# The first two modulation rows moved from TensorE to VectorE, stepped from the third attention's projections on, and five weight buffers instead of six

## The chip, the cores and the metric

One core of a Trainium2 chip runs the kernel. The metric is the device time of one execution in microseconds (us); the kernel before takes 2123.35 us, the median of three runs from 2120.63 to 2124.16 us. TensorE multiplies matrices into PSUM, VectorE and ScalarE do the elementwise work, GpSimd a few masks and small operations, and SyncE issues nearly all of the DMA transfers from one queue, in order.

## The reference, cut to what matters

Two stacks of two layers follow each other on one sequence of 256 tokens with 1024 channels. A layer of the first stack has a state-space branch, three attention branches and gates over them, and a SwiGLU feed-forward block. A layer of the second stack has a gated mixer, differential attention against 256 further context tokens, and a convolutional feed-forward block; its norms are shifted and scaled by "modulation" vectors. What the change touches is how these vectors are computed. They depend on nothing but two inputs, `c` and `c_ctx`, and on weights, so they can be computed at any time before the second stack:

```python
def adaln(cvec, w, b, n):
    m = jax.nn.silu(cvec) @ w[:, : n * D_MODEL] + b[: n * D_MODEL]
    return jnp.split(m, n, axis=-1)

for l in range(DEPTH):
    cmod = adaln(c_ctx, w_mod[l], b_mod[l], 2 if last else 6)
    sh1, sc1, g1, sh2, sc2, g2 = [m[:, None, :] for m in adaln(c, w_mod[l], b_mod[l], 6)]
```

For each of two layers that is a product of two vectors of 1024 (one for the latent tokens, one for the context) with a matrix of 1024 x 6144, in six rows of 1024 outputs.

## The kernel before, in words

All large products run in three passes over operands that are split into a high and a low half (`mm3`, lines 508 to 510). The weights come as a stream of units of at most 128 x 1024 numbers, 512 KB (`Stream`, lines 245 to 292): `_load` (line 258) issues the DMA on SyncE's queue into one of `RAW` = 6 buffers named raw, `_split` (line 266) makes the high half hi on ScalarE (line 275) and the low half lo on VectorE (line 277), each in one of four buffers, and TensorE then multiplies. The load is thus queued until the low half of the unit six places before has been made.

Work that isn't on the main line of projections is written as generators. `run_side` (line 475) takes one step of each of the "lanes" (the attention branches and the like) between projections. The modulation is one more generator, `mods` (line 1117), advanced by `fill` (line 493); `spread` (line 500) counts steps and calls `fill` at each `every`-th of them, while fewer than `goal` fills are done. A tile scheduler then orders the instructions of each engine by a simulated clock, with the order of writing as the priority, so an instruction may run far ahead of its place in the code.

`mods` goes through 6 rows x 8 steps for each layer. A step loads 128 x 1024 modulation weights, 512 KB, into one of two buffers named wm (line 1141, SyncE's queue, one step ahead). Rows 0 and 1 of the first layer, called early, are summed on TensorE: four matmuls a step with 32 columns each, of which two are not zero, into four groups of PSUM partitions (line 1159), over eight steps. All other rows are summed on VectorE, in two halves of 512 and for each of the two vectors (one vector in the last rows of the second layer): first a product (line 1170), then seven multiply-adds (line 1172) into a tile macc. `mod_end` (line 1183) finishes a row: for the rows of VectorE TensorE first sums macc over the partitions by eight matmuls with a vector of ones (line 1190); then for every row a copy, two transposes (line 1198) and an addition of the bias (line 1202), in later steps.

In `first_layer` (line 625) for l = 0 the sixteen steps of the early rows are advanced at each second gate product (lines 750 and 751), four for each of four gates, and two more steps, the first two of row 2, behind the gates (lines 774 and 775). The second layer's norm needs rows 0 and 1 first in `ctx_norm` (line 1604), right behind. The feed-forward block and the output product then take a step at every second unit. The third attention is the branch with the projections fq, fk and fv (lines 701 to 703).

Of the kernel before, what the change touches and what calls it, by code (L numbers as in the profile page):

```python
# [9 lines left out]
F32 = mybir.dt.float32  # L10
FR = mybir.dt.float32r
AF = mybir.ActivationFunctionType
ALU = mybir.AluOpType
# [13 lines left out]
UNIT = 1024  # L27
GROUP = {n: g for g, ns in (("a", "sm p pt dp at on yo osq"), ("c", "cth lj cn"), ("g", "gz gsq gu ga"), ("m", "mo"))
         for n in ns.split()}
KEEP = 1154 + 4 + 64 + 2 * (280 + 80 + 96 + 48)  # L30
LIM = 2.4e19
# [264 lines left out]
class Kern:  # L296
    RAW = 6
    CPINS = (None, None, None, 0, None, None, None, 1)
# [16 lines left out]
    SIDE2 = 5  # L315
    MSTEP = 1
    WM = 2
# [7 lines left out]
    def __init__(self, nc, tc, ctx, dr, stop=None):  # L325
        self.nc, self.tc, self.dr = nc, tc, dr
        self.stop = stop
        e = ctx.enter_context
        self.cp = e(tc.tile_pool(name="const", bufs=1))
        self.wp = e(tc.tile_pool(name="wts", bufs=4))  # L330
        self.sp = e(tc.tile_pool(name="slots", bufs=self.NSLOT))
        self.tp = e(tc.tile_pool(name="tmp", bufs=3))
        self.mp = e(tc.tile_pool(name="psmm", bufs=4, space=PSUM))
        self.ap = e(tc.tile_pool(name="psax", bufs=4, space=PSUM))
        self.dp = e(tc.tile_pool(name="scratch", bufs=1, space=bass.MemoryType.DRAM))
        self.x = self.cp.tile([128, 2, D], F32, name="x")
        self.xc = self.cp.tile([128, 2, D], F32, name="xc")
        cpk = const_params()
        kept = self.cp.tile([128, cpk.n + KEEP], F32, name="kept")
        self.kept, self.kept_n = kept, 0  # L340
        self.ident, cst, self.tabs, self.ctp, self.ct, self.ones, self.nh, self.par_f = (
            self.keep(n) for n in (128, cpk.n, 512, 256, 16, 1, 1, 240))
        self.cst_all, self.cst = cst, {n: cpk.get(cst, n) for n in cpk.at}
        for t in range(2):
            for h in range(2):
                sl = slice(512 * h, 512 * h + 512)
                nc.sync.dma_start(self.x[:, t, sl], dr["x"][128 * t:128 * t + 128, sl])
        nc.sync.dma_start(self.ident, dr["ident"])
        nc.gpsimd.memset(self.ones, 1.0)
        nc.gpsimd.memset(self.nh, -0.5)  # L350
        self.par = {}
        self.uid = 0
        self.lanes = [[] for _ in range(7)]
        self.front = []
        self.P2, self.late, self.ctx_out, self.tails = None, [], {}, []
        self.filler, self.filled = None, 0
        self.steps, self.every, self.goal = 0, 0, 51
        layers = [(dr[f"w_f{l}"], first_units(l)) for l in range(2)] + [(dr[f"w_s{l}"], second_units(l)) for l in range(2)]
        self.st = Stream(self, layers)
# [114 lines left out]

    def run_side(self, n=1):
        for lane in self.lanes:
            for _ in range(n):
# [48 lines left out]
    def proj_N(self, key, acts, width, k0=0, per=2, side=1, kbs=None, ps=None, last=True, held=0, pins=()):  # L526
# [25 lines left out]
        for kb in kbs[:len(kbs) - held]:  # L552
            some(self.st.next(key + (k0 + kb,)), kb, range(nt))
            self.run_side(side)
            self.spread()
        if held:
# [68 lines left out]
    def first_layer(self, x, x4, l, done=None):  # L625
        nc = self.nc
# [60 lines left out]
        for n, (a, b, c) in ((3, ("dq", "dk", "dv")), (2, ("mq", "mk", "mv"))):  # L687
# [11 lines left out]
            lane.append(g)  # L699
            ys[n] = (y, g)  # L700
        qT = direct("fq", -0.125)
        kT = direct("fk", 1.0)
# [36 lines left out]
        for n in (3, 2, 1, 0):  # L739
            y, g = ys.pop(n)  # L740
            gt = [self.slot("gt") for _ in range(2)]
            for m in range(8):
# [6 lines left out]
                self.run_side(2)  # L749
                if l == 0 and m % 2:  # L750
                    self.fill(1)
                if m == 6:
# [6 lines left out]
            for m in range(4):  # L759
# [12 lines left out]
                self.run_side(2)  # L772
                self.fill(self.BRF)
        while self.filled < 18:
            self.fill(1)
# [28 lines left out]
    def ffn_in(self, hT, part, fn, side=1):  # L804
# [7 lines left out]
        for i, m in enumerate(part):  # L812
# [12 lines left out]
            self.run_side(side)  # L825
            self.spread()
        return hid
# [289 lines left out]
    def mods(self, l):  # L1117
        nc, dr = self.nc, self.dr
        if l == 0:
# [4 lines left out]
            nc.vector.tensor_scalar(self.ct, th, 0.5, None, op0=ALU.mult)  # L1124
            nc.gpsimd.memset(self.ctp, 0.0)
            self.onep = self.keep(64)
            nc.gpsimd.memset(self.onep, 0.0)
            nc.gpsimd.memset(self.onep.rearrange("p (w m) -> p w m", m=32)[:, 0, 0:1], 1.0)
            nc.gpsimd.memset(self.onep.rearrange("p (w m) -> p w m", m=32)[:, 1, 1:2], 1.0)
            nc.vector.tensor_copy(self.ctp.rearrange("p (k m) -> p k m", k=8)[:, :, 0:2], self.ct.rearrange("p (k w) -> p k w", k=8))  # L1130
        bm = self.keep(48)
# [13 lines left out]
        for i, (r, k) in enumerate(units):  # L1145
            next(last, None)
            nw = 2 if l == 0 or r < 2 else 1
            while len(loaded) <= min(47, i + self.MSTEP):
                load()
            early = l == 0 and r < 2  # L1150
            if k == 0 and early:
                ps = self.ax_ps("am")
            if early:
                if (k + 1) % self.MSTEP:
                    yield
                    continue
                for kk in range(k + 1 - self.MSTEP, k + 1):
                    for j in range(4):
                        nc.tensor.matmul(ps[32 * j:32 * j + 32, :256], self.ctp[:, 32 * kk:32 * kk + 32],  # L1159
                                         loaded[i - k + kk][:, 256 * j:256 * j + 256], start=kk == 0, stop=kk == 7,  # L1160
                                         skip_group_check=True, tile_position=(0, 32 * j))
            else:
                if k == 0:
                    sums = [self.wp.tile([128, UNIT], F32, tag="macc", name=f"macc{l}_{r}_{w}", bufs=2) for w in range(nw)]
                for h in range(2):
                    o = slice(512 * h, 512 * h + 512)
                    for w in range(nw):
                        c = self.ct[:, 2 * k + w:2 * k + w + 1]
                        if k == 0:
                            nc.vector.tensor_scalar(sums[w][:, o], loaded[i][:, o], c, None, op0=ALU.mult)  # L1170
                        else:
                            nc.vector.scalar_tensor_tensor(sums[w][:, o], loaded[i][:, o], c, sums[w][:, o],  # L1172
                                                           op0=ALU.mult, op1=ALU.add)
            if k < 7:
                yield
                continue
            last = self.mod_end(l, r, nw, bm, md, ps if early else None, None if early else sums)
            next(last)
# [3 lines left out]

    def mod_end(self, l, r, nw, bm, md, ps, sums):
        nc = self.nc
        if sums is not None:
            yield
            ps = self.ax_ps("am")
            for w in range(nw):
                for j in range(4):
                    nc.tensor.matmul(ps[32 * j:32 * j + 32, :256], self.onep[:, 32 * w:32 * w + 32],  # L1190
                                     sums[w][:, 256 * j:256 * j + 256], start=w == 0, stop=w == nw - 1,
                                     skip_group_check=True, tile_position=(0, 32 * j))
        mo = self.tmp("mo", 256)
# [639 lines left out]
```

## Time and profile before

| | us |
|---|---|
| median of three runs | 2123.35 |
| lowest and highest | 2120.63, 2124.16 |
| the profiled execution | 2122.26 |
| its span, from the first to the last instruction | 2120.5 |
| TensorE busy with matmuls | 2068.8 |
| VectorE busy | 1550.2 |
| ScalarE busy | 1044.9 |
| mean granted share of TensorE's clock | 0.987 |

The profile is one execution, taken by the hardware profiler. Busy is the time in which an engine ran at least one instruction; a matmul's end is modelled and the next one starts before it, so the starts of matmuls tell more than their durations. PE stands for TensorE, PEld for its weight loads, DVE for VectorE, ACT for ScalarE, POOL for GpSimd, SP for SyncE, and a q behind a name for the engine's queue. L1159 is line 1159. `am<-wm,kept` says that the instruction writes the tile am and reads wm and kept.

### The profile page before, as it was taken

What the parts mean: (1) busy time and instruction counts of PE and PEld (TensorE: products, weight loads), DVE (VectorE), ACT (ScalarE), POOL (GpSimd) and SP (SyncE); (2) the same over time, 40 slices, a digit from 0 to 9 for tenths busy, and PEclk for the clock granted to TensorE, in tenths of its full rate; (3) what the DMA queues carried; (4) which work ended last, traced back from release to release, by engine and by line L of the source; (5) the groups of instructions that cost most, each with busy time, mean ns of one, the idle gap of its engine ahead of it and who ended that gap; (6) DMA issues with size and microseconds to landing.
All of it is one profiled execution on the core that took longest, in us unless ns stands there. A gap on an engine that the chain in (4) does not pass through costs nothing.

```text
span 2120.5 us, 34093 instructions
## 1 busy us (share of the span) xinstructions
PE 2068.8 (98%) x13092; PEld 1802.5 (85%) x13092; DVE 1550.2 (73%) x2957; ACT 1044.9 (49%) x1840; POOL 107.4 (5%) x137
## 2 busy tenths in 40 slices
PE   8999999999999999999999998999999999998999
PEld 6788899899887889998899887687888888878997
DVE  7856656899679566658988579689558656977774
ACT  5555644644455556456456454553313434455552
POOL 0001100100020011000000001000000000200000
PEclk9999999999999999999999999799999999999999
DMA  8545566587755454466754655156357343324562
GB/s 313 159 140 179 170 196 228 184 278 250 238 169 177 137 165 154 140 181 215 240 160 159 210 175 163 58 162 196 105 184 238 122 137 120 97 83 149 184 212 93
DMA packets 102356, 366.67 MB, mean 173 GB/s; under 512 B 12512, under 2 KB 12720, under 8 KB 102192
## 3 DMA queue, kind: packets, MB, share of 16 engines
q1 hardware_dynamic: 99920, 358.65, 52.4%
q0 software_dynamic: 2272, 5.83, 0.9%
q8 instruction: 103, 1.69, 0.3%
q14 instruction: 61, 0.50, 0.1%
HBM read 361.76 MB, written 2.68 MB: 172 GB/s over the span
## 4 chain that ended last, share of the span: by engine, by line
PE 90%; DVE 7%; issue 1%; ACT 1%; DMA 0%; SPq 0%; POOL 0%; POOLq 0%; DVEq 0%; ACTq 0%
PE mm L508 27%; PE mm L510 27%; PE mm L509 26%; PE ax L1328 2%; DVE lo L277 2%; PE ax L936 1%; DVE macc L1172 1%; PE ax L1358 1%; DVE yp L1519 1%; PE ay L591 1%; PE am L1159 1%; ACT hi L275 1%; PE ax L891 1%; PE am L1190 1%; PE ay L456 1%
## 5 line engine op out<-in xcount | busy, mean ns | idle before, releaser
L275 ACT ACTIVATE hi<-raw 128x1024 fp32r<-128x1024 f32 (+1 forms) x564 | 593.9, 1055 | 770.5 <-PE mm L509 354.2
L277 DVE TENSOR_TENSOR lo<-raw,hi 128x1024 fp32r<-128x1024 f32 (+1 forms) x564 | 684.6, 1215 | 371.2 <-ACT hi L275 354.6
L508 PE MATMUL mm<-hThi,hi 128*128 128x256 f32 (+1 forms) x2408 | 723.6, 303 | 7.9 <-DVE th L1567 3.0
L509 PE MATMUL mm<-hTlo,hi 128*128 128x256 f32 (+1 forms) x2408 | 720.0, 300 | 0.5 <-DVE hTlo L466 0.5
L510 PE MATMUL mm<-hThi,lo 128*128 128x256 f32 (+1 forms) x2408 | 717.7, 299 | 0.0
L508 PEld LDWEIGHTS mm<-hThi,hi 128*128 128x128 f32 x2408 | 460.2, 192 | 39.0 <-issue 17.9
L509 PEld LDWEIGHTS mm<-hTlo,hi 128*128 128x128 f32 x2408 | 462.3, 192 | 16.7 <-issue 2.8
L510 PEld LDWEIGHTS mm<-hThi,lo 128*128 128x128 f32 x2408 | 461.2, 192 | 17.6 <-issue 3.3
L508 PE MATMUL mm<-hi,hThi 128*128 128x512 f32 (+2 forms) x480 | 180.3, 385 | 1.4 <-ACT hThi L465 1.0
L509 PE MATMUL mm<-lo,hThi 128*128 128x512 f32 (+2 forms) x480 | 180.8, 378 | 0.0
L510 PE MATMUL mm<-hi,hTlo 128*128 128x512 f32 (+2 forms) x480 | 179.8, 377 | 0.4 <-DVE hTlo L466 0.2
L509 PE MATMUL mm<-lo,hh 128*128 128x512 f32 x440 | 171.5, 390 | 0.0
L510 PE MATMUL mm<-hi,hl 128*128 128x512 f32 x440 | 171.1, 389 | 0.0
L508 PE MATMUL mm<-hi,hh 128*128 128x512 f32 x440 | 170.4, 391 | 0.0
L1172 DVE SCALAR_TENSOR_TENSOR macc<-wm,kept,macc 128x512 f32<-128x512 f32 x224 | 158.3, 742 | 16.0 <-DMA wm<-in_w_mod 16.0
L508 PEld LDWEIGHTS mm<-hi,hThi 128*128 128x128 f32 x480 | 90.2, 189 | 22.1 <-issue 4.4
L510 PEld LDWEIGHTS mm<-hi,hTlo 128*128 128x128 f32 x480 | 90.5, 189 | 16.8 <-DVE hTlo L466 0.9
L509 PEld LDWEIGHTS mm<-lo,hThi 128*128 128x128 f32 x480 | 90.6, 189 | 15.4 <-issue 0.7
L508 PEld LDWEIGHTS mm<-hi,hh 128*128 128x128 f32 x440 | 82.6, 188 | 17.9 <-issue 0.8
L509 PEld LDWEIGHTS mm<-lo,hh 128*128 128x128 f32 x440 | 82.6, 188 | 17.9 <-issue 0.8
L510 PEld LDWEIGHTS mm<-hi,hl 128*128 128x128 f32 x440 | 82.6, 188 | 17.3
L1519 DVE SCALAR_TENSOR_TENSOR yp<-yp,kept 128x256 f32<-128x256 f32 x180 | 80.1, 475 | 0.2
(353 smaller groups left out, 2609.2 us busy)
## 6 DMA issues: line engine op xcount, KB each, us to landing
raw<-in_w_f SPq DMA_DIRECT2D x364, 512.0 KB, 3.7
raw<-in_w_s SPq DMA_DIRECT2D x190, 512.0 KB, 4.1
wm<-in_w_mod SPq DMA_DIRECT2D x96, 512.0 KB, 4.5
bc<-csd POOLq DMA_DIRECT2D x32, 128.0 KB, 5.8
mrow<-md SPq DMA_DIRECT2D x6, 512.0 KB, 4.3
row<-in_rows SPq DMA_DIRECT2D x4, 512.0 KB, 5.4
raw<-in_w_f SPq DMA_DIRECT2D x4, 510.0 KB, 5.1
par<-in_par_s SPq DMA_DIRECT2D x2, 918.5 KB, 8.3
```

The source lines that it names most:

```text
L275: nc.scalar.activation(hi[:, :n], raw[:, :n], AF.Copy)
L277: nc.vector.tensor_sub(lo[:, :n], raw[:, :n], hi[:, :n].bitcast(F32))
L456: nc.tensor.transpose(pss[k // 2][:, o:o + 128], xs[k // 4][:, 128 * (k % 4):128 * (k % 4) + 128], self.ident)
L508: nc.tensor.matmul(ps, ah, bh, start=first, stop=False)
L509: nc.tensor.matmul(ps, ah, bl, start=False, stop=False)
L510: nc.tensor.matmul(ps, al, bh, start=False, stop=last)
L591: nc.tensor.transpose(ps[:, b * 256 + t * 128:b * 256 + t * 128 + 128], nat[t][:, (b0 + b) * 128:(b0 + b) * 128 + 128], self.ident)
L891: nc.tensor.matmul(pair[j][:, 128:384], q[j][:, 128:], k[j], start=True, stop=True)
L936: nc.tensor.matmul(ps[64 * j:64 * j + 64, 0:256], vv, pt[:, 0:256], start=True, stop=False, skip_group_check=True)
L1172: nc.vector.scalar_tensor_tensor(sums[w][:, o], loaded[i][:, o], c, sums[w][:, o], op0=ALU.mult, op1=ALU.add)
L1328: nc.tensor.matmul(both[m][:, 256 * j:256 * j + 256], qT[64 * m:64 * m + 64, 256 * h + 128 * t:256 * h + 128 * t + 128], kT[64 * m:64 * m ...
L1519: nc.vector.scalar_tensor_tensor(c, y[:, j:j + 256], wj, c, op0=ALU.mult, op1=ALU.add)
```

## The change

Rows 0 and 1 of the first modulation layer are summed on VectorE as all others are, so the TensorE branch, the padded vectors `ctp` and the parameter `MSTEP` go, and each of the two rows ends with the eight matmuls of ones. The sixteen steps and the two behind them are no longer tied to the gate products: from the third attention's projections to the end of the gates every fourth call of `run_side` takes a step, and `spread` isn't called elsewhere meanwhile. There are 4 such calls in each of fq, fk and fv, 8 and 4 in the next two groups of projections and 12 in each of the four gates, so the eighteenth step comes with the first branch product of the last gate. `RAW` is 5 instead of 6, and the kept area is 256 columns smaller.

```diff
-KEEP = 1154 + 4 + 64 + 2 * (280 + 80 + 96 + 48)
+KEEP = 1154 - 256 + 4 + 64 + 2 * (280 + 80 + 96 + 48)
-    RAW = 6
+    RAW = 5
-    MSTEP = 1
...
     def run_side(self, n=1):
+        if self.early:
+            self.spread()
         for lane in self.lanes:
...
             self.run_side(side)
-            self.spread()
+            if not self.early:
+                self.spread()
...
+        if l == 0:
+            self.every, self.goal, self.early = 4, 18, True
         qT = direct("fq", -0.125)
...
                 self.run_side(2)
-                if l == 0 and m % 2:
-                    self.fill(1)
...
+        if l == 0:
+            self.every, self.goal, self.early = 0, 51, False
         while self.filled < 18:
             self.fill(1)
...
-            nc.gpsimd.memset(self.ctp, 0.0)
...
-            nc.vector.tensor_copy(self.ctp.rearrange("p (k m) -> p k m", k=8)[:, :, 0:2], self.ct.rearrange("p (k w) -> p k w", k=8))
...
-            early = l == 0 and r < 2
-            if k == 0 and early:
-                ps = self.ax_ps("am")
-            if early:
...
-                for kk in range(k + 1 - self.MSTEP, k + 1):
-                    for j in range(4):
-                        nc.tensor.matmul(ps[32 * j:32 * j + 32, :256], self.ctp[:, 32 * kk:32 * kk + 32],
-                                         loaded[i - k + kk][:, 256 * j:256 * j + 256], start=kk == 0, stop=kk == 7,
-                                         skip_group_check=True, tile_position=(0, 32 * j))
-            else:
-                if k == 0:
-                    sums = [self.wp.tile([128, UNIT], F32, tag="macc", name=f"macc{l}_{r}_{w}", bufs=2) for w in range(nw)]
+            if k == 0:
+                sums = [self.wp.tile([128, UNIT], F32, tag="macc", name=f"macc{l}_{r}_{w}", bufs=2) for w in range(nw)]
+            for h in range(2):
+                o = slice(512 * h, 512 * h + 512)
+                for w in range(nw):
+                    c = self.ct[:, 2 * k + w:2 * k + w + 1]
+                    if k == 0:
+                        nc.vector.tensor_scalar(sums[w][:, o], loaded[i][:, o], c, None, op0=ALU.mult)
+                    else:
+                        nc.vector.scalar_tensor_tensor(sums[w][:, o], loaded[i][:, o], c, sums[w][:, o],
+                                                       op0=ALU.mult, op1=ALU.add)
...
-    def mod_end(self, l, r, nw, bm, md, ps, sums):
+    def mod_end(self, l, r, nw, bm, md, sums):
         nc = self.nc
-        if sums is not None:
-            yield
-            ps = self.ax_ps("am")
...
+        yield
+        ps = self.ax_ps("am")
+        for w in range(nw):
+            for j in range(4):
+                nc.tensor.matmul(ps[32 * j:32 * j + 32, :256], self.onep[:, 32 * w:32 * w + 32],
+                                 sums[w][:, 256 * j:256 * j + 256], start=w == 0, stop=w == nw - 1,
+                                 skip_group_check=True, tile_position=(0, 32 * j))
```

## Rows read from the trace of the kernel before

**Rows 1.** The page: busy us of the engines, share of the span, instructions.
```profile
PE 2068.8 (98%) x13092; PEld 1802.5 (85%) x13092; DVE 1550.2 (73%) x2957; ACT 1044.9 (49%) x1840; POOL 107.4 (5%) x137
```
**Rows 2.** The chain of waits from 90 to 370 us, by line.
```profile
by line: PE mm L508 28.1%; PE mm L510 26.5%; PE mm L509 25.9%; PE ax L936 4.5%; PE am L1159 4.0%; PE ax L891 1.6%; PE ax L889 1.5%; PE ax L939 1.4%; PE ax L1087 1.2%; PE ax L921 1.0%; PE ax L923 0.9%; PE ax L922 0.9%; PE ax L1102 0.6%; PE a
```
**Rows 3.** Stretches: length, busy PE, PEld, DVE, ACT, POOL, clock, DMA share, GB/s.
```profile
0.00:30.00 30.00, 21.51 (x105) 18.16 (x105) 18.24 (x60) 18.08 (x39) 3.61 (x16) 1.00 0.95 358
30.00:90.00 60.00, 60.00 (x302) 46.92 (x301) 56.04 (x159) 30.80 (x50) 2.22 (x3) 1.00 0.64 203
90.00:360.00 270.00, 269.24 (x2101) 237.19 (x2100) 158.34 (x329) 143.62 (x277) 13.93 (x21) 1.00 0.55 177
420.00:540.00 120.00, 120.00 (x1000) 117.31 (x1000) 113.59 (x176) 55.20 (x85) 6.45 (x6) 1.00 0.80 264
1395.00:1445.00 50.00, 46.47 (x279) 39.96 (x277) 44.46 (x94) 19.79 (x32) 1.09 (x2) 0.97 0.52 158
```
**Rows 4.** Line 1159: shortest, median, longest ns, first and last start us, form.
```profile
L1159 PE MATMUL am<-wm,kept x128: 379/379/404, 29.5 to 354.1; 128*32 128x256 f32 x128
```
**Rows 5.** The same line alone in a stretch: length, busy PE, busy PEld, clock, DMA.
```profile
90.00:370.00 280.00, 12.41 (x112) 3.09 (x112) 1.00 0.56 179
```
**Rows 6.** TensorE's timeline: start us, busy us, instruction, at a double and a small group.
```profile
219.11 1.07 PE L1159 MATMUL am<-wm,kept 128*32 128x256 f32 x16
...
293.51 0.28 PE L509 MATMUL mm<-hTlo,hi 128*128 128x256 f32 x1
293.63 0.28 PE L510 MATMUL mm<-hThi,lo 128*128 128x256 f32 x1
293.83 0.64 PE L1159 MATMUL am<-wm,kept 128*32 128x256 f32 x8
...
294.63 0.28 PE L509 MATMUL mm<-hTlo,hi 128*128 128x256 f32 x1
```
**Rows 7.** TensorE's timeline at the end of a row summed on VectorE.
```profile
445.87 1.06 PE L1190 MATMUL am<-macc,kept 128*32 128x256 f32 x12
```
**Rows 8.** VectorE's sums macc: shortest, median, longest ns, first and last start us.
```profile
L1172 DVE SCALAR_TENSOR_TENSOR macc<-wm,kept,macc x224: 720/743/754, 358.0 to 1709.8; 128x512 f32<-128x512 f32 x112
...
L1170 DVE TENSOR_SCALAR macc<-wm,kept x32: 468/480/561, 352.4 to 1690.5; 128x512 f32<-128x512 f32 x32
```
**Rows 9.** VectorE's timeline at two moments of the first 30 us.
```profile
9.93 1.22 DVE L277 TENSOR_TENSOR lo<-raw,hi 128x1020 fp32r<-128x1020 f32 x1 [0.27 <-ACT hi L275]
...
28.60 0.17 DVE L641 TENSOR_SCALAR hb<-kept 128x32 f32<-128x32 f32 x1
```
**Rows 10.** Waits from 1395 to 1445 us: us in total, times, longest.
```profile
PE mm L508 <- DVE th L1567: 3.0, 1, 3.0
```
**Rows 11.** GpSimd's groups from 90 to 370 us: busy us, mean ns, idle before.
```profile
L1022 POOL TENSOR_SCALAR_AFFINE_SELECT dg<-bc 128x1024 f32<-128x1024 f32 x4 | 4.3, 1092 | 30.9 <-PE ax L939 30.9
```
**Rows 12.** Waits of SyncE's DMA queue, whole run: us in total, times, longest.
```profile
SPq L262 <- DVE lo L277: 1106.4, 370, 14.1
SPq L1141 <- DVE macc L1172: 87.3, 51, 5.4
```
**Rows 13.** The weight buffers raw from 420 to 540 us: instructions, and DMA time to landing.
```profile
L262 SPq DMA_DIRECT2D raw<-in_w_f x42: 327/328/638, 420.0 to 538.7; - x42
L275 ACT ACTIVATE hi<-raw x41: 1057/1061/1064, 419.2 to 539.3; 128x1024 fp32r<-128x1024 f32 x41
L277 DVE TENSOR_TENSOR lo<-raw,hi x41: 1205/1218/1226, 421.5 to 537.5; 128x1024 fp32r<-128x1024 f32 x41
...
DMA to landing us min/median/max: 3.5/4.5/6.3
```
**Rows 14.** ScalarE's timeline at 24 us; in brackets the idle time before, and its releaser.
```profile
24.52 1.06 ACT L275 ACTIVATE hi<-raw 128x1024 fp32r<-128x1024 f32 x1 [2.84 <-DMA raw<-in_w_f]
```
**Rows 15.** SyncE's timeline: the sixth load of weights.
```profile
7.79 0.66 SPq L262 DMA_DIRECT2D raw<-in_w_f  x1
```
**Rows 16.** TensorE's timeline behind a group of line 1159.
```profile
254.65 0.66 PE L1087 MATMUL ax<-dg,xdt 128*64 128x128 f32 x8 [0.76 <-DVE dg L1078]
```

More of the change, by code (lines that the diff above doesn't have):

```diff
@@ L340, in __init__ @@
         self.kept, self.kept_n = kept, 0
-        self.ident, cst, self.tabs, self.ctp, self.ct, self.ones, self.nh, self.par_f = (
-            self.keep(n) for n in (128, cpk.n, 512, 256, 16, 1, 1, 240))
+        self.ident, cst, self.tabs, self.ct, self.ones, self.nh, self.par_f = (
+            self.keep(n) for n in (128, cpk.n, 512, 16, 1, 1, 240))
         self.cst_all, self.cst = cst, {n: cpk.get(cst, n) for n in cpk.at}
@@ L356, in __init__ @@
         self.filler, self.filled = None, 0
-        self.steps, self.every, self.goal = 0, 0, 51
+        self.steps, self.every, self.goal, self.early = 0, 0, 51, False
         layers = [(dr[f"w_f{l}"], first_units(l)) for l in range(2)] + [(dr[f"w_s{l}"], second_units(l)) for l in range(2)]
@@ L825, in ffn_in @@
             self.run_side(side)
-            self.spread()
+            if not self.early:
+                self.spread()
         return hid
@@ L1147, in mods @@
             nw = 2 if l == 0 or r < 2 else 1
-            while len(loaded) <= min(47, i + self.MSTEP):
+            while len(loaded) <= min(47, i + 1):
                 load()
-            early = l == 0 and r < 2
-            if k == 0 and early:
-                ps = self.ax_ps("am")
-            if early:
-                if (k + 1) % self.MSTEP:
-                    yield
-                    continue
-                for kk in range(k + 1 - self.MSTEP, k + 1):
-                    for j in range(4):
-                        nc.tensor.matmul(ps[32 * j:32 * j + 32, :256], self.ctp[:, 32 * kk:32 * kk + 32],
-                                         loaded[i - k + kk][:, 256 * j:256 * j + 256], start=kk == 0, stop=kk == 7,
-                                         skip_group_check=True, tile_position=(0, 32 * j))
-            else:
-                if k == 0:
-                    sums = [self.wp.tile([128, UNIT], F32, tag="macc", name=f"macc{l}_{r}_{w}", bufs=2) for w in range(nw)]
[L1165 to L1173, printed above, removed]
+            if k == 0:
[9 more added lines that the diff above has]
+                                                       op0=ALU.mult, op1=ALU.add)
             if k < 7:
@@ L1176, in mods @@
                 continue
-            last = self.mod_end(l, r, nw, bm, md, ps if early else None, None if early else sums)
+            last = self.mod_end(l, r, nw, bm, md, sums)
             next(last)
@@ L1181, in mods @@
             yield
-    def mod_end(self, l, r, nw, bm, md, ps, sums):
+    def mod_end(self, l, r, nw, bm, md, sums):
         nc = self.nc
-        if sums is not None:
-            yield
-            ps = self.ax_ps("am")
[L1188 to L1192, printed above, removed]
+        yield
[5 more added lines that the diff above has]
+                                 skip_group_check=True, tile_position=(0, 32 * j))
         mo = self.tmp("mo", 256)
```

## The prediction, made before the changed kernel ran

> **What bounds the kernel now.** I read the page first, then the chain of waits by stretches, then the busy time by stretches, and last the instructions of the modulation one by one. The page gives TensorE 2068.8 us of the 2120.5 us span [rows 1], but matmuls are pipelined, so that alone would not do. The chain of waits from 90 to 370 us, the stretch in which nearly all of the moved work lies, runs over TensorE's projections for four fifths, and 4.0% of it, 11 us, stands on line 1159, the matmuls that the change takes away [rows 2]. In the busy times TensorE is never free in that stretch (269.24 of 270 us), while VectorE works 158.34 of 270 us, so 112 us of it lie idle [rows 3]. The granted clock is 1.00 in all of it, the 2.4 GHz level. So this stage is paced by TensorE, and VectorE has room.
>
> **What goes from TensorE.** Each of the 16 steps of rows 0 and 1 is four matmuls, two records each: 128 records, from 29.5 to 354.1 us [rows 4], 112 of them after 90 us [rows 5]. Their median of 379 ns must not be multiplied by 128 (48.5 us): the four write four column groups and run together. Alone they cover 12.41 us of the stretch [rows 5], one group of sixteen records covers 1.07 us, and a group of two to eight, as the one of eight shown, 0.62 to 0.64 us [rows 6], so there are (12.41 - 1.07) / 0.63 = 18 small groups and one double one; the 16 records before 90 us are three more. What a group costs is read from its neighbours: the matmul before it starts at 293.63, the second one behind it at 294.63, which is 1.00 us for two matmuls that elsewhere follow at 0.12 us (293.51 to 293.63), so 1.00 - 0.24 = 0.76 us [rows 6]. The double group is 1.07 - 0.64 = 0.43 us longer, 1.19 us. Sum after 90 us: 18 x 0.76 + 1.19 = 14.9 us; the three early ones 2.3 us.
>
> **What comes to TensorE.** Two rows more end as the later rows do, by 16 matmuls with the ones vectors, which sum the partitions. Such a row stands in the trace as a group of twelve records, 1.06 us busy, so 0.76 + 0.42 = 1.18 us [rows 7], and one of four some 4 us behind it, like the small ones, 0.76 us: 1.94 us a row, 3.9 us for two. The copy, transposes and the add behind it stay as they are. Net 14.9 - 3.9 = 11.0 us after 90 us. I take the three early groups as worth nothing (they stand where TensorE waits for the first weights and the index chain anyway) and keep 2.3 us as the other end: 11.0 to 13.3 us.
>
> **What comes to VectorE.** Sixteen steps of four instructions, 64: 8 are the first products at 480 ns and 56 the multiply-adds at 743 ns [rows 8], 3.8 + 41.6 = 45.4 us. That hides in the 112 idle us as a sum; whether it hides in order of time is the question. The planner orders each engine's queue by a simulated clock and pulls ready work far ahead: the second layer's half gate bias, line 641, runs at 28.60 us, hundreds of us before its layer [rows 9]. So I expect the multiply-adds to run as soon as their weights have landed and VectorE is free, which from 30 to 90 us it hardly is (56.04 of 60 [rows 3]), and then to fill it nearly whole from 90 us on: at 41% idle, 45 us of work fill some 110 us. Queued behind each are the low halves of the weights (line 277) and the softmax; a step holds them up by 4 x 0.74 = 3 us at most. The nearest row is 420 to 540 us, the same kind of step at VectorE 113.59 of 120 us, and there TensorE has no gap (120.00) [rows 3]: cost 0, which I take. The other end is 1395 to 1445 us, the stretch where steps fill VectorE and TensorE does stop, 46.47 of 50 us, with 3.0 us on one result of VectorE [rows 3, 10]; 3.53 / 50 over 120 us is 8.5 us. The first product of a row waits until TensorE has read the row before; that wait is 3.7 us at the longest now, twice more, on an engine with room.
>
> The Trainium skill, "SBUF — State Buffer", section "Who interferes with whom", speaks against the move: a VectorE instruction with two SBUF inputs, which the multiply-add is, contends with a GpSimd instruction that reads SBUF, and whoever comes second waits for the whole of the other. GpSimd's four mask instructions of 1.09 us lie in this stage [rows 11]; by that rule and if each held up the chain in full, the sum would be 4 x 1.09 = 4.4 us worse, still faster; no row before shows the two side by side.
>
> **The DMA queue and five buffers.** The 16 loads of modulation weights are the same, on SyncE's queue among the weight loads, only earlier; a queued load waits for VectorE instead of TensorE, and the weight loads behind it wait too. Now such waits for the steps sum to 87.3 us in 51 cases, 5.4 us at the longest; the weight loads themselves wait mostly for the last reader of their buffer, 1106.4 us, so the ring is full nearly always [rows 12]. What one buffer less takes away is worked out where units go by fastest, 42 loads in 120 us, 2.86 us each: five buffers are 14.3 us, less 1.06 + 1.22 us for the two splits and 6.3 us for the slowest landing leaves 5.7 us, an estimate [rows 13]. Cost 0 there. Only in the first 30 us, where the DMA engines are 0.95 busy [rows 3], does a split wait for its weights, 2.84 us [rows 14]; the sixth load must there wait for the end of the first low half (9.93 + 1.22 = 11.15 us instead of 7.79 us [rows 9, 15]). Bounds: 3.4 us lost, or 1.5 us won, since the loads behind come 512 KB earlier at 358 GB/s [rows 3]; I take 0. The two steps of row 2 that now end the stage come a few us sooner; no cost.
>
> **Sum.** The profiled execution took 2122.26 us for a span of 2120.5 us, and the median of the runs is 2123.35 us, 1.1 us more. 2122.3 - 11.0 = 2111.3 us, as a median 2112 us. Ends: 2122.3 - 13.3 - 1.5 = 2107.5 and 2122.3 - 11.0 + 8.5 + 3.4 = 2123.2 us.
>
> **Rivals.**
> First, the groups were fillers. Ten of the 22 groups lie at or before 254 us, among attention work, where the planner put them because it saw TensorE waiting; at 254.65 us TensorE even waits 0.76 us for VectorE behind one [rows 16]. If those places stay empty, only the twelve groups between gate matmuls count: 12 x 0.76 - 3.9 = 5.2 us, 2118 us. For it: that row. Against it: it is the only such gap, and gate and value projections are at hand to fill. Chance 0.15.
> Second, VectorE becomes the bound from 90 to 210 us as from 1395 to 1445 us: 8.5 us back, 2122.3 - 11.0 + 8.5 = 2119.8, as a median 2121 us, no difference that shows. For it: VectorE's queue is in order and the plan leaves it no slack to catch up. Against it: 420 to 540 us. Chance 0.18.
> Third, slower: five buffers with the modulation loads in the same queue let the splits run dry. The place is a load of modulation weights that stands ahead of weight loads and waits for a late step; the cushion of 5.7 us is just over the longest wait now, 5.4 us. From about seven waits that reach TensorE at the mean of 87.3 / 51 = 1.7 us, the gain is gone. There would be some 51 + 12 waits; if a quarter (16) reach it, 27 us are lost: 2122.3 - 11.0 + 27 = 2138 us. For it: VectorE is fuller. Against it: outside the first 30 us splits wait for TensorE to free their buffers, not for weights. Chance 0.12.
>
> **How the numbers follow.** The forecast, 2112 us, has 0.55, with 2108 to 2116 of its own. The range takes in the fillers and the second rival and leaves the third out: 2107 to 2122 us. A measurement of this kernel tells about 0.2%, 4.2 us, from no change, so faster is below 2119.1 us: the forecast, and the fillers for the most part, 0.70; within 0.2%: the second rival and the rest, 0.18; slower: 0.12.
>
> **What would show it.** Right: no records on line 1159, 64 more first products and multiply-adds of the sizes above, most of them between 90 and 250 us; six rows summed over the partitions for the first modulation layer instead of four; TensorE without gaps from 90 to 360 us and the end of the gates some 11 us earlier, while everything behind it only shifts. The fillers: the same start but gaps or slow pitches around the attention matmuls. The second: VectorE near full from 90 to 210 us and TensorE waiting for softmax or low halves. The third: ScalarE's splits waiting for weight DMAs outside the first 30 us. I am wrong if the stages behind 400 us change by more than 2 us, for I give them nothing.

## The result: 28 us slower, and the profile after

The changed kernel takes 2150.3 us (median of four runs, 2149.6 to 2151.2) beside 2122.2 us before: 1.0128 times the time, 95% interval 1.0116 to 1.0140. The prediction was 2112 us with a range up to 2122 us. The profiled execution has a span of 2149.4 us, 28.9 us more than before. Line numbers have shifted: the first products and multiply-adds of the modulation are L1160 and L1162 now, the sums over partitions L1179, the weights' loads L1144.

The page of after, and then its stretches (busy us of PE, PEld, DVE, ACT and POOL, clock, DMA share, GB/s), for comparison with [rows 1, 3]:

```profile
PE 2068.3 (96%) x12996; PEld 1805.0 (84%) x12996; DVE 1591.9 (74%) x3020; ACT 1046.0 (49%) x1840; POOL 112.2 (5%) x136
```
```profile
0.00:30.00 30.00, 18.87 (x94) 15.95 (x95) 20.07 (x58) 18.78 (x38) 3.46 (x15) 1.00 0.95 360
30.00:90.00 60.00, 57.98 (x281) 45.98 (x280) 60.00 (x112) 26.53 (x35) 2.48 (x3) 1.00 0.74 241
90.00:360.00 270.00, 248.89 (x1840) 220.97 (x1839) 182.51 (x440) 135.53 (x276) 15.54 (x22) 0.93 0.48 152
420.00:540.00 120.00, 119.12 (x960) 114.40 (x959) 112.30 (x177) 59.44 (x96) 9.99 (x8) 1.00 0.72 242
1395.00:1445.00 50.00, 49.91 (x321) 44.84 (x321) 38.46 (x92) 26.10 (x50) 2.22 (x3) 1.00 0.41 134
```
VectorE now has no idle time from 30 to 90 us, and TensorE, which was free for less than 1 us from 90 to 360 us, is idle for 21 of these 270 us. A finer cut, at the places where TensorE stops, of after:

```profile
90.00:111.00 21.00, 20.54 (x140) 18.83 (x138) 21.00 (x42) 7.31 (x7) 0.00 (x0) 1.00 0.78 262
111.00:136.00 25.00, 6.81 (x31) 2.99 (x30) 22.33 (x69) 1.44 (x2) 0.65 (x1) 0.61 0.60 191
136.00:165.00 29.00, 28.62 (x160) 22.17 (x160) 14.03 (x61) 18.28 (x54) 0.05 (x1) 0.75 0.06 19
```
From 111 to 136 us TensorE works 6.8 us. Its timeline tells what it waits for (start us, busy us, instruction, idle time before and its releaser):

```profile
72.02 1.06 PE L1179 MATMUL am<-macc,kept 128*32 128x256 f32 x12
...
122.86 1.07 PE L1179 MATMUL am<-macc,kept 128*32 128x256 f32 x4 [11.70 <-DVE macc L1162]
...
133.03 1.01 PE L996 MATMUL ax<-kept 128*16 128x256 f32 x2 [5.49 <-issue]
...
135.79 0.93 PE L894 MATMUL ax<-dk,dq 64*128 64x128 f32 x3
```
The sums of row 0 are read at 72.02 us; the wait of 11.70 us is for those of row 1 on VectorE. The next one, labelled "issue", ends right behind the last value that the small scan for the state-space branch writes on VectorE (L990, at 132.77 us below), which L996 reads. Behind these come, at 135.79 us, the first scores of the attention that uses the index selection (L894); before the change they started at 72.96 us. VectorE's instructions on macc up to 165 us (count, shortest, median and longest ns, first and last start), and its timeline around 123 us:

```profile
L1162 DVE SCALAR_TENSOR_TENSOR macc<-wm,kept,macc x60: 653/746/790, 23.3 to 130.7; 128x512 f32<-128x512 f32 x60
...
L1160 DVE TENSOR_SCALAR macc<-wm,kept x12: 469/477/480, 20.2 to 127.5; 128x512 f32<-128x512 f32 x12
```
```profile
122.06 1.41 DVE L1162 SCALAR_TENSOR_TENSOR macc<-wm,kept,macc 128x512 f32<-128x512 f32 x2 [2.15 <-DMA wm<-in_w_mod]
...
123.46 0.28 DVE L878 MATCH_REPLACE8 isc<-m,isc 128x128 f32<-128x128 f32 x1
123.65 1.40 DVE L1162 SCALAR_TENSOR_TENSOR macc<-wm,kept,macc 128x512 f32<-128x512 f32 x2
...
132.77 0.16 DVE L990 SCALAR_TENSOR_TENSOR kept<-kept,a 128x16 f32<-128x16 f32 x1
...
134.98 0.40 DVE L882 TENSOR_TENSOR sel<-sel,kept 128x256 f32<-128x256 f32 x1
```
All eighteen steps' 72 instructions run from 20 to 131 us, woven into the index selection of the first layer: rounds of MAX8 (the eight largest scores) and MATCH_REPLACE (strike them out), one behind the other, that end with the mask sel. It ends at 135.4 us; before, its last instruction started at 75.33 us and ended at 75.7 us. Of the 60 us in between, 42.2 + 5.2 us are these steps and 15.6 us low halves of weights (30 of them from 20 us to the end of the selection instead of 17); VectorE was idle for 4.6 us of that time before and for 2.5 us in after, 2.15 us of it for the load of modulation weights in the brackets above. So neither of TensorE's two long waits is for the mask itself: row 1's sums, the small scan and the selection all pass through VectorE, and all of them are late.

**Where the 28.9 us are.** The next table numbers the 11232 projection matmuls (those that write mm), which all kernels run in the same count, and tells how much later (+) or earlier a kernel starts one of them than the kernel before, each in its profiled execution. The number is in brackets in the head, and the times there are those of before; "selection" to "gates" are the stages with the moved work, 1272 to 1863 us holds the first attention of the second stack, 1863 to 1952 us its second. The first two columns count projections alone: at the 400th, after has 80 other matmul records behind it and before has 159, so its -7.5 us there is no gain; from 273 us on the other matmuls are level again in after.

| kernel | median us | 115 us (400) | 129 us (500) | 273 us (1300) | 367 us (2000) | 1272 us (7400) | 1863 us (9800) | 1952 us (10100) |
|---|---|---|---|---|---|---|---|---|
| after | 2150.3 | -7.5 | +35.2 | +33.0 | +23.8 | +20.8 | +24.3 | +29.0 |
| e1_five | 2131.1 | +0.6 | +0.6 | +0.3 | +0.3 | +0.3 | +3.9 | +8.1 |
| e3_place_only | 2116.6 | -0.7 | -0.7 | +6.2 | -2.7 | -3.7 | -3.1 | +1.5 |
| e4_vector_at_gates | 2150.9 | -6.0 | +35.3 | +31.5 | +22.4 | +21.3 | +25.2 | +29.8 |
| e5_behind_index | 2134.7 | -4.9 | -4.1 | +11.6 | +2.4 | +3.1 | +5.9 | +12.1 |
| e6_behind_index_six | 2132.6 | -5.8 | -4.7 | +19.3 | +10.2 | +6.7 | +3.7 | +10.4 |
| e7_few_multiply_adds | 2119.6 | +5.8 | +5.8 | +1.6 | -7.6 | -7.9 | -2.1 | -1.9 |
| e8_in_place_five | 2120.7 | -2.3 | -2.3 | +2.8 | -4.2 | -4.7 | -2.6 | +2.4 |
| e8_in_place_six | 2129.4 | -2.5 | -2.5 | +2.2 | -4.8 | -5.2 | -0.8 | +5.1 |
| e9_split_five | 2121.6 | -5.3 | -4.6 | -0.1 | -7.1 | -8.5 | -5.0 | -0.4 |
| e9_split_six | 2131.0 | -6.6 | -5.6 | +0.2 | -6.8 | -9.9 | -3.2 | +10.3 |
| e10_four | 2138.4 | +1.4 | +1.4 | +1.4 | +1.4 | +1.2 | +3.7 | +16.0 |
| e10_seven | 2124.3 | -1.5 | -1.5 | -1.6 | -1.6 | -2.9 | -0.8 | -0.7 |
| e11_third_gate_five | 2115.5 | -4.9 | -4.2 | -3.7 | -10.4 | -12.3 | -5.8 | -5.3 |
| e11_third_gate_six | 2112.1 | -6.8 | -5.8 | -4.9 | -11.6 | -12.8 | -9.8 | -9.5 |

Behind 1952 us nothing changes any more. Each row is a single execution: that of e3_place_only took 2123.7 us, 7.1 us more than its median, that of e8_in_place_five 4.0 us more than its median. The first row has the change: 33 us are lost between 111 and 165 us, 9.2 us come back in the gates (the gain that was forecast), and the second stack's attention adds 3.5 and 4.7 us. Of the 33, idle TensorE is 18.2 us from 111 to 136 us and 2.0 us from 30 to 90 us; low clock, reckoned as busy time x (1 - granted clock), is 6.81 x 0.39 + 28.62 x 0.25 = 9.8 us, an estimate. Together that is 30.0 us; the rest is not attributed. The clock is at 1.00 up to 111 us and falls to the lower level (0.50 from 120 to 150 us) in the long stop.

The columns at 1272 and 1952 us have one thing in common for all rows: between them each of the 15 kernels loses time against before, 2.2 to 20.2 us. So a new plan cost something there in every profiled execution, whatever had been changed; for e3_place_only that hangs on the one execution profiled.

### The profile page after: what moved, and what is told of

Its sections match the earlier page's. It is cut to its first block, busy times and chain, and to the rows that moved or that the text cites. A ratio compares the mean times of both kernels' runs of the same rounds, so it can differ in the third digit from the quotient of the medians.

```text
span 2149.4 us, 34040 instructions
## 1 busy us (share of the span) xinstructions
PE 2068.3 (96%) x12996; PEld 1805.0 (84%) x12996; DVE 1591.9 (74%) x3020; ACT 1046.0 (49%) x1840; POOL 112.2 (5%) x136
## 4 chain that ended last, share of the span: by engine, by line
PE 89%; DVE 7%; issue 1%; ACT 1%; DMA 1%; SPq 0%; POOLq 0%; DVEq 0%
PE mm L509 27%; PE mm L510 26%; PE mm L511 26%; DVE macc L1162 2%; PE ax L1317 2%; DVE lo L277 2%; PE ax L941 1%; PE ax L1347 1%; PE am L1179 1%; PE ax L896 1%; PE ay L593 1%; DVE yp L1508 1%; PE ax L894 1%; PE ax L1337 1%; PE ay L455 1%
## 5 line engine op out<-in xcount | busy, mean ns | idle before, releaser
L1162 DVE SCALAR_TENSOR_TENSOR macc<-wm,kept,macc 128x512 f32<-128x512 f32 x280 | 198.2, 745 | 16.8 <-DMA wm<-in_w_mod 16.7
L509 PE MATMUL mm<-hi,hThi 128*128 128x512 f32 (+2 forms) x480 | 175.9, 382 | 2.3 <-ACT hThi L464 1.9
```

Source lines behind the costliest of these rows:

```text
L509: nc.tensor.matmul(ps, ah, bh, start=first, stop=False)
```

## The experiments

Theory H: the planner pulls the multiply-adds, whose weights are there early, into the index selection, a serial chain on VectorE that TensorE waits for. Rival R: five buffers starve the splits (the prediction's third rival). Rival P: it is the new place of the steps, not the engine. The ratios below are against the kernel before as it ran beside each: 2123.95 us for e1 to e5, 2122.3 us for e6 to e8, 2122.6 us for e9 and e10, 2123.26 us for e11.

**The ring alone.** The kernel before with
```diff
-    RAW = 6
+    RAW = 5
```


> The kernel before with five weight buffers instead of six and nothing else. Theory H (the planner runs the new multiply-adds inside the first layer's index selection, from 20 to 131 us, and the attention behind it comes 60 us late): no difference beyond 0.3%, 2116 to 2128 us, since no multiply-add has moved. Rival R (five buffers starve the stream of weights): most of the loss is here, 2140 to 2150 us, with splits on ScalarE that wait for DMAs. Rival P (the place of the steps and the early loads do it): 2122 us as H.


2131.1 us, 1.0040 (1.0026 to 1.0054). Five buffers alone cost 7.1 us (8.1 us in the table; the later expectations say 8.9, against the 2122.2 us of the result). H had wanted no difference and R most of the loss, so both missed and R isn't empty. But they lie behind 1272 us, not where R had the splits starve, and cannot explain the 33.

**The place alone.** The kernel before, with its rows on TensorE and six buffers, stepped as in the change:
```diff
+        if l == 0:
+            self.every, self.goal, self.early = 4, 18, True
         qT = direct("fq", -0.125)
...
-                if l == 0 and m % 2:
-                    self.fill(1)
```


> The kernel before with its two rows on TensorE and six buffers, but the steps called as in the change, at every fourth side step from the third attention's projections on. H: 2116 to 2128 us, because TensorE has no free time in the plan into which the matmuls would be pulled, and VectorE gets nothing. R: 2122 us. P: 2140 to 2150 us.


2116.6 us, 0.9978 (0.9965 to 0.9991), a little faster; its ten runs lie from 2114.2 to 2125.5 us. P is out.

**The engine alone.** The changed kernel (VectorE rows, five buffers) with the steps at the gates as before, the reverse of the diff above.


> The changed kernel with two rows on VectorE and five buffers, but the steps called where the kernel before calls them, at every second gate product. H: the place of writing hardly matters, because whatever is ready is pulled ahead, so again late index selection and 2140 to 2160 us. R: 2140 to 2150 us as well. P: the gain of the forecast, 2110 to 2116 us.


2150.9 us, 1.0131 (1.0115 to 1.0146), the same as the change, and the selection ends at 137.7 us. Where the code writes the steps doesn't matter: the planner takes them ahead all the same.

**Behind the selection.** The changed kernel with one edge, so that no VectorE instruction of the eighteen steps is queued ahead of the selection's last:
```diff
+            self.front = [self.sel_ins]
...
-            nc.vector.tensor_max(sel[:, o], sel[:, o], self.cst["causal"][:, o])
+            self.sel_ins = nc.vector.tensor_max(sel[:, o], sel[:, o], self.cst["causal"][:, o]).ins
```


> The changed kernel with one edge more: VectorE's instructions of the first eighteen steps are queued behind the last instruction of the first layer's index selection (the maximum with the causal mask). Five buffers, the same steps. H: index selection ends near 73 us as before, no multiply-add stands ahead of it, and the 11 us of TensorE's work are won: 2106 to 2118 us. R: 2140 us or more, since the ring is the same. P: 2140 us or more, since place and loads are the same.


2134.7 us, 1.0056 (1.0041 to 1.0071). The stop at 111 us is gone and 15.6 of the 28 us come back, so H has the larger part. But H had expected more. The stretches of e5 show what is late next; before, TensorE was never idle in them:

```profile
150.00:180.00 30.00, 28.45 (x220) 23.39 (x218) 21.58 (x57) 18.28 (x41) 4.35 (x8) 1.00 0.51 159
180.00:210.00 30.00, 28.46 (x231) 26.01 (x235) 30.00 (x53) 11.41 (x17) 3.76 (x2) 1.00 0.70 223
210.00:240.00 30.00, 24.44 (x175) 19.40 (x168) 24.20 (x100) 17.43 (x51) 0.00 (x0) 0.89 0.49 163
```
Row 1's steps and the two behind them come bunched (157 to 219 us), VectorE is full from 180 to 210 us, and the softmax is late: TensorE's waits from 150 to 245 us (us in total, times, longest) begin with

```profile
PE ax L927 <- DVE p L921: 4.4, 2, 3.0
PE mm L511 <- DVE lo L277: 2.2, 1, 2.2
```
That is the kind of the prediction's second rival, at its end and behind it, and at 15.7 us by the table (129 to 273 us) instead of 8.5.

**The same with six buffers.**


> e5_behind_index with six weight buffers. Theory now: the change's loss has three terms: the planner pulls the multiply-adds into the first layer's index selection (gone here as in e5), the ring of five (8.9 us in e1_five, gone here), and VectorE full at 170 to 240 us (some 12 us in e5, stays). So 2134.7 - 8.9 = 2126 us (2122 to 2129). Rival ring: the later stages differ from plan to plan and five buffers are not the cause: 2131 to 2137 us. Rival queue: the sixth buffer also ends the stall at 170 to 240 us, since the loads wait there for a buffer: 2111 to 2118 us.


2132.6 us, 1.0047 (1.0032 to 1.0062): 2.1 us less than with five, not 8.9, and the loss from 129 to 273 us is larger with six (24.0 us), not smaller. So the theory (the ring's 8.9 us) and the rival of the queue missed; the time lies in the range of the rival by which five buffers are not the cause, but not only the later stages differ: by the table six buffers lose 7.7 us more up to 273 us and get most of it back behind.

**VectorE's work taken away, all else kept.** The changed kernel, but in rows 0 and 1 of the first modulation layer only the last of the seven multiply-adds is made, so 35.7 us of VectorE's work are left out:
```diff
-                    else:
+                    elif l or r > 1 or k == 7:
                         nc.vector.scalar_tensor_tensor(sums[w][:, o], loaded[i][:, o], c, sums[w][:, o],
```


> The changed kernel without 48 of the 56 multiply-adds of rows 0 and 1 of the first modulation layer (the steps k = 1 to 6; the first products, the last multiply-adds, all loads, all sums over partitions and five buffers stay), so these rows are not the reference's. 48 x 0.743 = 35.7 us of VectorE's work less, nearly all of it from 20 to 130 us. Theory (VectorE's time in the index selection is the loss): the selection ends some 30 to 36 us sooner, 2150.3 - 33 = 2117 us (2112 to 2124). Rival, the loads: it is the sixteen early loads in SyncE's queue and their waits, and VectorE's time is only beside it: 2140 us or more.


2119.6 us, 0.9985 (0.9975 to 0.9994). All loads, sums and five buffers are still there, and 31 us are gone; the selection ends at 87.8 us. The loads' waits for these multiply-adds went with them: from 15 to 136 us the loads of modulation weights wait 19.8 us for macc in after and 3.6 us here. But VectorE itself was busy for 112.9 of the 115.4 us from 20 us to the end of the selection in after, and idle for a load in 2.15 us of them. So it is VectorE's time in the selection, not the loads in SyncE's queue. That much of H is shown from both sides, by e5, which puts the multiply-adds behind the selection, and by e7, which leaves them out. That TensorE waits for the selection is more than these runs show: in the trace it waits for row 1's sums and for the small scan, which come late with it.

**In place.** The changed kernel with each step queued behind the newest VectorE instruction of the main line at its place in the code: first the selection, then xbc, z and the gates' branch products:
```diff
+                a = nc.vector.scalar_tensor_tensor(acc[:, s:], u[:, :256 - s], cw[:, 4 * m + j:4 * m + j + 1], acc[:, s:],
...
+            if l == 0:
+                self.front = [a.ins]
             self.run_side()
```


> Six weight buffers, and each of the sixteen steps' VectorE instructions is queued behind the newest instruction of the main line on VectorE at its place in the code (first the index selection, then the last instruction written of xbc, of z, and of each gate's branch product), so that none runs ahead. Theory: VectorE has 112 idle us from 90 to 360 us and the 45 us fit if they are not bunched; TensorE gains what the gates gained in the other runs, 9 to 11 us, and nothing else changes: 2122 - 10 = 2112 us (2107 to 2117). Rival V: 45 us more on VectorE delay its work for TensorE wherever they stand, the twelve us seen in e5 at 170 to 240 us stay: 2121 to 2127 us.

> The same as e8_in_place_six with the change's five weight buffers. Ring theory: 8.9 us (as in e1_five) above e8_in_place_six, 2121 us (2117 to 2126). Rival: the same as with six within 3 us.


2129.4 us with six buffers (1.0032, 1.0021 to 1.0043) and 2120.7 us with five (0.9995, 0.9985 to 1.0004). Both expectations missed, though the number with five lies in the range of its ring theory: that theory had five slower than six, and five are 8.8 us faster here. At 273, 367 and 1272 us the two agree within 0.6 us, and both lose some 7 us from 257 to 273 us.

**Row 0 early, row 1 in the gates.** The edges of e8, and no step between the two rows:
```diff
-            self.every, self.goal, self.early = 4, 18, True
+            self.every, self.goal, self.early = 1, 8, True
...
+            if l == 0 and n == 2:
+                self.every, self.goal = 3, 18
             y, g = ys.pop(n)
```


> Six weight buffers. Row 0's eight steps are taken at the eight calls in fq and fk, queued on VectorE behind the index selection; row 1's eight steps and two more are taken at every third call from the second gate on, each queued behind the newest branch product of the gates. So no multiply-add stands in the state-space branch from some 150 to 270 us, where e8 lost 6.6 us (from 4.4 us ahead to 2.2 behind) and e5 12 us. Theory place (the loss that stays in e8 comes from multiply-adds beside the state-space branch): 4 us ahead at 230 us as in e8, no stop from 238 to 273 us, 7 us more in the gates: 2122 - 11 = 2111 us (2106 to 2117, the later stages vary by some 5 us from plan to plan). Rival V: 45 us on VectorE cost the same wherever they stand, a new stop from 80 to 150 us or in the gates takes the 6 us: 2117 to 2127 us.

> The same as e9_split_six with five weight buffers. Ring theory (a ring of five costs some 9 us as in e1_five): 2120 us. Scatter theory (e8 was 8.8 us faster with five than with six, e5 2.1 us slower: what differs is the plan of the second stack's attention stages, not the ring): 9 us to either side of e9_split_six, and the stages up to 1270 us within 1 us of it.


2131.0 us with six buffers (1.0036, 1.0023 to 1.0049) and 2121.6 us with five (0.9997, 0.9987 to 1.0007). Six missed both of its ranges. Five are 9.3 us faster, about what the scatter theory gives; the ring theory has the number only because it took six to be at 2111 us. In the table's columns up to 1272 us the two differ by at most 1.4 us. The stop at 170 us is away, that at 250 us remains. VectorE's timeline of e9_split_five:

```profile
247.96 1.27 DVE L776 SCALAR_TENSOR_TENSOR mg<-gt,mm 128x512 f32<-128x512 f32 x2
249.15 1.67 DVE L1169 TENSOR_SCALAR macc<-wm,kept 128x512 f32<-128x512 f32 x4
250.74 0.69 DVE L1073 TENSOR_TENSOR xdt<-ax,kept 128x512 f32<-128x512 f32 x1
...
251.42 0.68 DVE L1092 TENSOR_TENSOR dg<-dg,ax 128x512 f32<-128x512 f32 x1
```
and TensorE's:
```profile
252.15 1.12 PE L1101 MATMUL ax<-dg,xdt 128*64 128x128 f32 x8 [3.74 <-DVE dg L1092]
```
Row 1's first step stands directly behind the branch product it was tied to, and ahead of what the state-space branch needs. TensorE's wait for dg, 0.76 us before [rows 16], is 3.74 us (3.75 us in e9_split_six), and the clock falls.

**Other ring sizes.** The kernel before with `RAW = 7` and `RAW = 4`.


> The kernel before with seven weight buffers instead of six, nothing else. Ring theory: more buffers can only help, 2115 to 2122 us. Scatter theory: the stages up to 1270 us within 1 us of before, and from there up to 9 us to either side; slower than 2124 us would speak for it.

> The kernel before with four weight buffers. By the cushion of the prediction each buffer is worth one pitch of 2.86 us: five had 5.7 us over the slowest landing, four have 2.9 us, so where units go by fastest still no loss, and in the first 30 us another 1 to 3 us: 2123 to 2127 us by that, with the scatter of the second stack's attention 2115 to 2135 us. Ring theory: twice e1_five's loss or more, 2140 us and up, spread over the stages with fast weights.


2124.3 us with seven (1.0004, 0.9995 to 1.0014) and 2138.4 us with four (1.0074, 1.0057 to 1.0090). Seven bring nothing, so the ring theory missed; the profiled execution is 1.5 to 2.9 us ahead up to 1272 us, more than the 1 us of the scatter theory. Four buffers cost 1.2 us up to 1272 us, as the cushion of the prediction has it, and then 14.8 us in the second stack's attention; the time lies between the ranges of the two theories.

**Row 1 one gate later.** As e9, but row 1 begins at `n == 1` instead of `n == 2`, at every second call instead of every third:
```diff
+            if l == 0 and n == 1:
+                self.every, self.goal = 2, 18
```


> As e9_split_six, but row 1's steps begin with the third gate, at every second call, queued behind the second gate's branch product. In e9_split_five the first step of row 1 stands on VectorE at 249.15 us ahead of dg and TensorE waits for dg 3.74 us instead of 0.76 us [the row of the timeline], and 240 to 273 us lose 4 us. Theory D (these 4 us are the step in front of dg): no wait of over 1 us for dg, some 4 us ahead at 273 us and 10 to 12 us at 367 us; with the scatter of the second stack's attention (e9 lost 17 us of 1272 to 1952 us with six and 8 with five) 2110 to 2125 us. Rival F (fillers: without TensorE's groups there is a gap there, whatever VectorE does): the loss at 238 to 273 us stays 3 us or more, 7 us ahead at 367 us as in e9.

> The same as e11_third_gate_six with five weight buffers. Theory D and rival F as there, the same within 1 us up to 367 us. Ring theory: later by more than 3 us at 1270 us; scatter theory: the same at 1270 us within 1.5 us, then up to 9 us to either side.


2112.1 us with six buffers (0.9944, 0.9929 to 0.9959) and 2115.5 us with five (0.9957, 0.9941 to 0.9974): both faster than before and than the change. In e11_third_gate_six VectorE goes from the branch product straight on,

```profile
247.19 1.27 DVE L776 SCALAR_TENSOR_TENSOR mg<-gt,mm 128x512 f32<-128x512 f32 x2
248.39 0.68 DVE L1073 TENSOR_TENSOR xdt<-ax,kept 128x512 f32<-128x512 f32 x1
248.99 0.68 DVE L1092 TENSOR_TENSOR dg<-dg,ax 128x512 f32<-128x512 f32 x1
```
and TensorE's wait for dg is
```profile
249.72 0.66 PE L1101 MATMUL ax<-dg,xdt 128*64 128x128 f32 x8 [2.08 <-DVE dg L1092]
```
Theory D had put this wait under 1 us; it is 2.08 us. But the loss from 238 to 273 us, which rival F wanted to stay, has gone: the kernel is 4.9 us ahead at 273 us and 11.6 us at 367 us. More than the 1.7 us of the wait itself has gone, and the rest shows in the clock behind it, at the lower level behind the longer wait and at the upper one behind the shorter; that the wait decides it is read from these rows, not tested. The stretch behind the wait, in e9_split_six and then in e11_third_gate_six:

```profile
252.00:258.00 6.00, 4.94 (x34) 4.10 (x29) 6.00 (x9) 1.04 (x3) 0.00 (x0) 0.57 0.42 135
```
```profile
252.00:258.00 6.00, 6.00 (x53) 5.50 (x48) 4.16 (x7) 0.86 (x3) 0.00 (x0) 1.00 0.57 165
```
With five buffers the kernel is 1.2 us behind that with six at 273 and at 367 us, where 1 us had been the limit, and 0.5 us at 1272 us, so the ring theory is out here.

## Why the prediction was wrong, step by step

**TensorE's term was right.** In after the gates give back 33.0 - 23.8 = 9.2 us; twelve small groups at 0.76 us were 9.1 us. In e11_third_gate_six, where the moved work stands neither in the selection nor in the state-space branch, the sum up to 367 us is 11.6 us, forecast 11.0. The first rival (fillers, 5.2 us) counted the gates' groups too, so the 9.2 us do not speak against it; the 4.9 us that e11_third_gate_six is ahead at 273 us, in front of these groups, do. But not all of the 11.6 us need come from the engine: e3_place_only is 2.7 us ahead at 367 us with its rows still on TensorE. That the time of 2112.1 us is just the forecast's is luck: it is made up of 12.8 us won up to 1272 us and 3.3 us lost behind, and with the five buffers of the change it is 2115.5 us.

**VectorE's size was right, its place wrong, and this step failed:** "so I expect the multiply-adds to run as soon as their weights have landed and VectorE is free, which from 30 to 90 us it hardly is, and then to fill it nearly whole from 90 us on", cost 0. Multiply-adds and first products take 746 and 477 ns as forecast (743 and 480 ns), but run from 20 to 131 us, and there they cost 33 us. The planner did not wait for VectorE to be free; it mixed them in, at a stage where VectorE was 0.93 busy [rows 3]. The prediction had even quoted the sign, an instruction of the second layer at 28.60 us [rows 9], and then summed idle time from 90 us on. And "a step holds them up by 4 x 0.74 = 3 us at most" treats each step by itself; a serial chain of some 50 instructions that is met by all eighteen steps is held up by all of them, 47.4 us. The row taken as nearest, 420 to 540 us, has no such chain on VectorE.

**The rivals.** The second, VectorE as the bound, was the mechanism, but its place was 90 to 210 us and its price 8.5 us from the stretch of 1395 us; it is 33 us at 111 to 165 us. The third, dry splits, didn't happen: in after no split on ScalarE waits for a weight load behind 30 us, and e7, which keeps all loads and five buffers, is 31 us faster.

**Five buffers** at cost 0 held for all stages up to 1272 us (e1_five +0.3 us, e10_four +1.2 us). The statement that stages behind 400 us change by no more than 2 us did not hold (-3.0, +3.5, +4.7 us in after). Whether the ring causes that isn't settled: five against six buffers is +7.1 us (e1), +2.1 (e5, e6), -8.8 (e8), -9.3 (e9) and +3.4 (e11) in the medians, so between two plans these stages differ by up to 9 us to either side. Against before they were slower in all 15 profiled executions; why its plan is the fastest there is not shown.

**The contention** that the prediction weighed, by the Trainium skill, "SBUF — State Buffer", section "Who interferes with whom", had next to no part in after, where the multiply-adds were done before the four masks it counted. Two smaller masks of the index selection met them, at 66.54 us, and took 1.63 and 0.72 us instead of 1.23 and 0.29. In e5 the large ones meet them; VectorE's and GpSimd's timelines of e5:

```profile
192.05 1.48 DVE L1163 SCALAR_TENSOR_TENSOR macc<-wm,kept,macc 128x512 f32<-128x512 f32 x1
```
```profile
189.22 3.76 POOL L1028 TENSOR_SCALAR_AFFINE_SELECT dg<-bc 128x1024 f32<-128x1024 f32 x2 [18.56 <-PE ax L945]
```
Two masks take 3.76 us instead of 2 x 1.09 [rows 11], and the multiply-add that starts in the second takes 1.48 us instead of 0.74, which agrees with that page of the Trainium skill: whoever comes second waits. At some 2 us it was not the cause. The prediction found no row before with a multiply-add beside a mask; a low half beside one, which also reads two tiles of SBUF, was in that trace, at 836.88 us, and there the mask took 2.01 us.

## What to carry to other kernels

Idle time summed over a stage says nothing of work that a planner is free to start earlier: ask when the inputs are first there, and what serial chain stands on that engine at that moment. Here the move needed edges that hold the moved work behind that chain, and a place for its steps where no other engine waits for a short result; with both it is 0.56% faster with six buffers and 0.43% with five, without them 1.28% slower. A ring of buffers should be judged by several plans, not by one pair, and a small gain in one stage against what a new plan costs in the others.

## What was not expected of the hardware

The second stack's last attention stage, from 1863 to 1952 us, takes 88.8 us in before and 94.7 us in e8_in_place_six, although TensorE, VectorE and ScalarE run the same instructions in the same order there (e10_seven, the same order too: 89.0 us). The executions compared here took 2122.3, 2127.3 and 2121.6 us. TensorE's timeline of before, and its next stretch:

```profile
1888.18 1.16 PE L1358 MATMUL ax<-vv,at 128*128 128x128 f32 x8 [1.37 <-ACT at L1350]
```
```profile
1890.00:1902.00 12.00, 11.91 (x59) 8.72 (x59) 8.47 (x20) 6.84 (x18) 0.00 (x0) 1.00 0.13 40
```
The same two of e8_in_place_six:
```profile
1889.53 1.16 PE L1354 MATMUL ax<-vv,at 128*128 128x128 f32 x8 [3.12 <-ACT at L1346]
```
```profile
1890.00:1902.00 12.00, 12.00 (x38) 7.59 (x37) 7.01 (x14) 4.90 (x12) 0.00 (x0) 0.57 0.01 1
```
A wait of 3.12 instead of 1.37 us, and behind it TensorE runs 12 us near the lower of its two levels (0.57) instead of at the upper (1.00): 38 records instead of 59. So in this stage, where short waits follow each other, a wait longer by 1.75 us goes with 5.9 us more in all. Single executions of one kernel differ by as much (e9_split_five 2119.1 to 2128.7 us), and with one profile of each it is not shown that the difference belongs to the plan and not to the execution. What lengthens the wait was not found out.
